# Strassen's scheme in a feed-forward net: seven block products for eight, with the second product run over all rows

## The chip, the cores and the metric

The kernel runs on one core of a Trainium2 chip. The core has five engines that work beside each other, each with its own queue of instructions: TensorE (PE, matrix products into the PSUM memory; PEld is its loading of the stationary operand), VectorE (DVE), ScalarE (ACT), GpSimd (POOL) and SyncE (SP), which here starts all DMA transfers. Data lies in SBUF, 128 partitions, and in PSUM, eight banks of 128 x 512 fp32. The metric is the device time of one execution in microseconds.

## The reference, cut to what matters

One layer on 1024 tokens of width 1024, all in float32: chunked attention and a convolution branch, gated and mixed, a layer norm, then a feed-forward net with a causal depthwise convolution of three taps inside it, and a second layer norm.

```python
def conv_ffn(x, w_up, w_dw, b_dw, w_down):
    u = x @ w_up
    a, b = jnp.split(u, 2, axis=-1)
    a = causal_dwconv(a, w_dw, b_dw)
    return (jax.nn.gelu(a) * b) @ w_down
...
        x = layer_norm(ALPHA * x + mix, ln1_g[l], ln1_b[l])
        ffn = conv_ffn(x, w_up[l], ffn_conv_w[l], ffn_conv_b[l], w_down[l])
        x = layer_norm(ALPHA * x + ffn, ln2_g[l], ln2_b[l])
```

`w_up` is 1024 x 5632 (2 x 2816) and `w_down` 2816 x 1024.

## The kernel before, in words

Float32 products are made of matmuls on a shorter format (fp32r). Each operand is split in two parts: `hi`, a copy on ScalarE into that format, and `lo`, the rest, by a subtraction on VectorE. A product of two blocks is three matmuls, hi x hi, hi x lo and lo x hi (`mm3`, L203 to L206). So all matmuls of the feed-forward net carry the lines L204 to L206, and every block that goes into one costs a copy and a subtraction. Weights come through two rings of raw blocks and of parts (`next_w`, L188 and L189), one block ahead.

`close_tile` makes the layer norm of 128 tokens: `take` adds a bank of the product to the residual `res[t]` (L687), `norm` does the rest (L691 to L710). Tile 7 has a form of its own, with statistics by an instruction of VectorE (L685, L691). `turn(h)` transposes the normed rows of a token half (L743) and splits them (L745, L746).

The feed-forward net follows. Its 22 column tiles f of 128 go in three groups. For each f there are two strips, a and b, each over both token halves with a depth of 8 blocks (`strip`); a gets the three taps (L789 to L791) and gelu (L792), b is multiplied in (L797), and the result is split into the parts `act`. After a group, its part of the down product is added to `res[t]` (L811). The last group closes the tiles: tiles 4 to 7 one after another, with tile 7's second half of columns in two pieces.

The order of the work on each engine isn't that of the lines. The program is given to a planner (`TileContext`), which issues on each engine whatever it expects to be ready, the earlier line first, and puts in the waits; within one engine the order is then fixed. SBUF ranges are handed out in program order by `Arena` (L58): it takes an end of a free range, preferring ranges that were not freed lately. An instruction that writes a range waits for the last reader of what lay there.

## Time and profile before

| | us |
|---|---|
| device time, median of 3 runs | 1447.89 |
| the runs | 1445.92, 1447.89, 1448.00 |
| profiled execution: span from its first to its last instruction | 1445.1 |
| TensorE busy in it | 1433.7 (99%) |
| VectorE, ScalarE, GpSimd busy | 752.9, 480.2, 3.9 |

The page gives the profiled execution no other time than its span; it is 2.8 us below the median of the runs. In rows of instruction groups stand line, engine, operation, output and inputs, count, then busy time, the mean of one in nanoseconds, and the engine's idle time before them with what ended it. In timelines the first number is the start and the second the length.

### The profile page before, as it was taken

To read this page: it belongs to the slowest core of one execution; us is meant where nothing else is said; L and a number is where in the kernel's file an instruction comes from. 1 tells how busy PE (TensorE), PEld (TensorE's weight loads), DVE (VectorE), ACT (ScalarE), POOL (GpSimd) and SP (SyncE) were. 2 spreads that over 40 slices of the span, in tenths; PEclk is the share of its full clock that TensorE was granted. 3 is DMA by queue.
4 is the path that set the end of the run, shared out by engine and by line. 5 is a ranking of instruction groups with operands and counts; after the bars stand their busy time and mean duration, and the time that the engine had idled before them with its cause. 6 is when DMAs were issued, how large, how long until landed. Compare 5 with 4: busy or idle time off the path is not lost.

```text
span 1445.1 us, 15551 instructions
## 1 busy us (share of the span) xinstructions
PE 1433.7 (99%) x6418; PEld 1160.1 (80%) x6418; DVE 752.9 (52%) x1149; ACT 480.2 (33%) x693; POOL 3.9 (0%) x27
## 2 busy tenths in 40 slices
PE   9999999999999999999999999999999999999997
PEld 8877777777778888888888888888888888888886
DVE  5288777786779955756643433213333312333438
ACT  4345455556662137322232222101222200122312
POOL 0000000000000000000000000000000000000000
PEclk9999999999999999999999999999999999999999
DMA  7011111111011111630011111111121111111302
GB/s 255 15 44 39 39 39 39 36 33 39 30 36 38 59 44 34 228 117 1 0 44 44 46 57 44 44 59 45 44 59 44 44 59 44 44 59 44 102 15 117
DMA packets 23285, 80.32 MB, mean 56 GB/s; under 512 B 2592, under 2 KB 2728, under 8 KB 23216
## 3 DMA queue, kind: packets, MB, share of 16 engines
...
q14 instruction: 19, 0.16, 0.0%
...
## 4 chain that ended last, share of the span: by engine, by line
PE 98%; DVE 1%; DMA 0%; ACT 0%; issue 0%; DVEq 0%
PE s L204 18%; PE s L205 18%; PE s L206 18%; PE mm L204 9%; PE mm L205 8%; PE mm L206 8%; PE s L430 2%; PE tp L455 2%; PE s L429 1%; PE tp L204 1%; PE tp L206 1%; PE tp L205 1%; PE pv L204 1%; PE pv L205 1%; PE pv L206 1%; PE pv L477 1%
## 5 line engine op out<-in xcount | busy, mean ns | idle before, releaser
L188 ACT ACTIVATE whi<-wraw 128x1024 fp32r<-128x1024 f32 x100 | 106.1, 1061 | 541.5 <-PE s L205 325.7
L189 DVE TENSOR_TENSOR wlo<-wraw,whi 128x1024 fp32r<-128x1024 f32 x100 | 122.1, 1221 | 310.4 <-ACT whi L188 310.0
L205 PE MATMUL s<-x1l,whi 128*128 128x512 f32 x704 | 274.3, 390 | 0.0
L204 PE MATMUL s<-x1h,whi 128*128 128x512 f32 x704 | 274.1, 390 | 0.0
L206 PE MATMUL s<-x1h,wlo 128*128 128x512 f32 x704 | 274.1, 389 | 0.0
L204 PE MATMUL mm<-xh,whi 128*128 128x512 f32 x384 | 164.3, 428 | 2.0 <-ACT qq L272 2.0
L204 PEld LDWEIGHTS s<-x1h,whi 128*128 128x128 f32 x704 | 132.1, 188 | 27.6 <-ACT x1h L745 0.3
L206 PEld LDWEIGHTS s<-x1h,wlo 128*128 128x128 f32 x704 | 132.2, 188 | 27.3
L205 PEld LDWEIGHTS s<-x1l,whi 128*128 128x128 f32 x704 | 132.1, 188 | 27.2
L412 DVE SCALAR_TENSOR_TENSOR acc<-hpad,par,acc 128x1024 f32<-128x1024 f32 x120 | 152.4, 1278 | 0.7
L206 PE MATMUL mm<-xh,wlo 128*128 128x512 f32 x384 | 151.9, 396 | 0.0
L205 PE MATMUL mm<-xl,whi 128*128 128x512 f32 x384 | 151.5, 394 | 0.0
L797 DVE TENSOR_TENSOR y<-y,s 128x1024 f32<-128x1024 f32 x22 | 26.9, 1221 | 129.1 <-PE s L206 129.1
L204 PEld LDWEIGHTS mm<-xh,whi 128*128 128x128 f32 x384 | 72.2, 188 | 21.7 <-issue 8.2
L206 PEld LDWEIGHTS mm<-xh,wlo 128*128 128x128 f32 x384 | 72.2, 188 | 15.5
L205 PEld LDWEIGHTS mm<-xl,whi 128*128 128x128 f32 x384 | 72.6, 189 | 9.1
L457 ACT ACTIVATE pth<-tp 128x512 fp32r<-128x512 f32 (+3 forms) x96 | 41.7, 434 | 65.2 <-PE tp L455 64.7
L458 DVE TENSOR_TENSOR ptl<-tp,pth 128x512 fp32r<-128x512 f32 (+3 forms) x96 | 46.9, 488 | 30.1 <-ACT pth L457 29.4
L438 ACT ACTIVATE p<-p,st 128x640 f32<-128x640 f32 (+2 forms) x64 | 44.4, 694 | 34.8 <-DVE st L436 34.2
L436 DVE CUSTOM_DVE_ANT_0 p<-s,bias 128x640 f32<-128x640 f32 (+2 forms) x64 | 41.8, 654 | 23.6 <-PE s L430 13.7
L204 PE MATMUL s<-xh,whi 128*128 128x512 f32 x128 | 49.8, 389 | 0.0
L205 PE MATMUL s<-xl,whi 128*128 128x512 f32 x128 | 49.8, 389 | 0.0
...
## 6 DMA issues: line engine op xcount, KB each, us to landing
wraw<-in_w_up SPq DMA_DIRECT2D x44, 512.0 KB, 3.4
wraw<-in_w_in SPq DMA_DIRECT2D x32, 512.0 KB, 3.4
wraw<-in_w_dn SPq DMA_DIRECT2D x22, 512.0 KB, 3.5
res<-in_x SPq DMA_DIRECT2D x8, 512.0 KB, 4.5
wraw<-in_w_o SPq DMA_DIRECT2D x8, 512.0 KB, 3.7
xraw<-in_xT SPq DMA_DIRECT2D x7, 512.0 KB, 7.6
out<-res SPq DMA_DIRECT2D x7, 512.0 KB, 2.6
...
```

What stands on the lines that cost most here:

```text
L188: S.activation(hi, raws[i], AF.Copy)
L189: V.tensor_sub(lo, raws[i], f32(hi))
L204: PE.matmul(o, ah, bh, start=first, stop=False)
L205: PE.matmul(o, ah, bl, start=False, stop=False)
L206: PE.matmul(o, al, bh, start=False, stop=last)
L412: V.scalar_tensor_tensor(a, hp[:, j:j + T], col(C_CW + c * TAPS + j), a, op0=OP.mult, op1=OP.add)
L430: PE.matmul(o[:, b, :w], ql[rs, qs], kk[rs, ks], start=False, stop=True)
L436: V.tensor_tensor_reduce(out=pv, in0=ov, in1=bv, scale=-0.125, scalar=3.0e38, op0=OP.add, op1=OP.min, accum_out=st[:, 0:1])
L438: S.activation(pt, pt, AF.Exp, bias=st[:, 0:1], scale=-1.0, accum_out=st[:, 1:2])
L455: PE.transpose(o[:, (i - i0) * P:(i - i0 + 1) * P], p_t[g][i - 4 * g][:, jj * P:(jj + 1) * P], ident)
L457: S.activation(ph[:, :w], o[:, :w], AF.Copy)
L458: last_lo[0] = V.tensor_sub(pl[:, :w], o[:, :w], f32(ph)[:, :w])
```

## The change

Each matrix of the two products is cut in two by two blocks, and a product of such matrices is made by Strassen's scheme in Winograd's form: seven block products on sums of blocks, and sums of the products. It is done on the blocks before the split into parts.

- The normed rows, transposed, are cut by depth (k blocks 0 to 3 and 4 to 7) and by token half. `turn0` makes the inputs of products 1 and 2 from the first token half, `turn1` those of 4, 5, 7, 6 and 3 from the second and from kept copies of the first. All seven stay in SBUF as parts, 112 KB per partition.
- Up: a `quad` is four weight blocks of 512 rows x 128 columns that belong together. GpSimd makes four sums of the next quad's weights (`prep_sums`), ScalarE and VectorE split weights and sums. Seven products of 12 matmuls follow; some add to the bank of an earlier one, after that one has been read. Results are combined on VectorE and GpSimd. Two quads give two column tiles of a and of b. The taps now read a from SBUF.
- GpSimd makes the four sums of the activations that the down product needs, and all seven inputs go to DRAM (`act_d`); so does the residual (`x1_d`).
- Down: seven products one after another, each over all rows, 11 steps of depth 128 with 12 matmuls each. Each step loads its activations from DRAM through a ring of six, and splits them and its weights (`step_parts`); GpSimd makes sums of weights in place and adds products to the residual. All eight tiles are closed late: tiles 4 to 7 after the sixth product, tiles 0 to 3 within the seventh.
- `close_tile` loses tile 7's own form. `_layout` packs the weights by quads (not shown).

The removed lines that are left out below are the loop over `GROUPS`, L778 to L841; some lines that free ranges are left out too.

```diff
@@ constants and plan @@
-GROUPS = ((0, 8), (8, 16), (16, FT))
+FP = FT // 2
...
-    for f0, f1 in GROUPS:
-        for f in range(f0, f1):
-            plan += [w_up[f], w_up[FT + f]]
-        if f1 < FT:
-            plan += [w_dn[c, f] for c in range(2) for f in range(f0 // 2, f1 // 2)]
-        else:
-            own |= set(range(len(plan), len(plan) + f1 - f0))
-            plan += [w_dn[c, f] for f in range(f0 // 2, f1 // 2) for c in range(2)]
...
@@ close_tile @@
-        r, st, last = res[t], st_r(), t == 7
+        r, st = res[t], st_r()
         m, v, y, z = (st[:, i:i + 1] for i in range(18, 22))
-        at = [0, 0]
-        def take(o):
-            i, a = at
-            n = o.shape[-1]
-            rc = r[:, a:a + n]
-            at[:] = i + 1, a + n
-            if last:
-                V.scalar_tensor_tensor(rc, rc, scale, o, op0=OP.mult, op1=OP.add)
-                V.bn_stats(st[:, 6 * i:6 * i + 6], rc)
+        def take(o, c, sign=None):
+            rc = r[:, cols[c]]
+            if sign is None:
+                V.scalar_tensor_tensor(rc, rc, scale, o, op0=OP.mult, op1=OP.add, accum_out=st[:, c:c + 1])
             else:
-                V.scalar_tensor_tensor(rc, rc, scale, o, op0=OP.mult, op1=OP.add, accum_out=st[:, i:i + 1])
+                V.scalar_tensor_tensor(rc, o, sign, rc, op0=OP.mult, op1=OP.add, accum_out=st[:, c:c + 1])
         def norm():
-            if last:
-                V.bn_aggr(st[:, 18:20], st[:, 0:6 * at[0]])
...
-            for c in cols if last else (slice(0, D),):
...
+            V.scalar_tensor_tensor(r, r, m, g_bc, op0=OP.subtract, op1=OP.mult)
+            V.scalar_tensor_tensor(r, r, y, b_bc, op0=OP.mult, op1=OP.add)
...
@@ build, after close_tiles @@
-    x1t = [[], []]
-    def turn(h):
+    xf = {}
+    xs = {}
+    def part(n):
+        xf[n] = [(sb(f"xfh{n}{i}", [P, HT], F32R), sb(f"xfl{n}{i}", [P, HT], F32R)) for i in range(4)]
+    def turned(o, h, k):
+        for i in range(4):
+            PE.transpose(o[:, toks[i]], res[4 * h + i][:, k * P:(k + 1) * P], ident)
+    def turn0():
+        for n in (1, 2):
+            part(n)
+            xs[n] = [sb(f"xs{n}{i}", [P, HT]) for i in range(4)]
         for k in range(KD):
+            n, i = 1 + k // 4, k % 4
             tp = bank()
-            for i in range(4):
-                PE.transpose(tp[:, toks[i]], res[4 * h + i][:, k * P:(k + 1) * P], ident)
-            hi, lo = sb(f"x1h{h}{k}", [P, HT], F32R), sb(f"x1l{h}{k}", [P, HT], F32R)
+            turned(tp, 0, k)
+            hi, lo = xf[n][i]
             S.activation(hi, tp, AF.Copy)
             V.tensor_sub(lo, tp, f32(hi))
-            x1t[h].append((hi, lo))
+            S.activation(xs[n][i], tp, AF.Copy)
+    def turn1():
+        for n in (4, 5, 7, 6, 3):
+            part(n)
+        for i in range(4):
+            o = bank2()
+            turned(o[:, 0], 1, i + 4)
+            turned(o[:, 1], 1, i)
+            x22, x5, x7, x6, x3 = (sb(f"xs{n}_{i}", [P, HT]) for n in (4, 5, 7, 6, 3))
+            S.activation(x22, o[:, 0], AF.Copy)
+            V.tensor_sub(x5, o[:, 1], x22)
+            V.tensor_sub(x7, xs[1][i], o[:, 1])
+            G.tensor_sub(x6, x5, xs[1][i])
+            G.tensor_add(x3, x6, xs[2][i])
+            for n, a in ((4, x22), (5, x5), (7, x7), (6, x6), (3, x3)):
+                hi, lo = xf[n][i]
+                S.activation(hi, a, AF.Copy)
+                V.tensor_sub(lo, a, f32(hi))
+            sb.free(x22, x5, x7, x6, x3)
+        sb.free(*xs[1], *xs[2])
+    quad_r, quads = [], []
+    wt = []
+    def load_quad():
+        q = len(quads)
+        if q < 2 * FP:
+            quads.append(quad_r[q % len(quad_r)])
+            nc.sync.dma_start(quads[-1], w_up[q])
+    def pair_of_parts(name, n):
+        return sb(name + "h", [P, n, HT], F32R), sb(name + "l", [P, n, HT], F32R)
+    def parts_of(dst, src):
+        hi, lo = dst
+        S.activation(hi, src, AF.Copy)
+        V.tensor_sub(lo, src, f32(hi))
+    def prep_raw(q):
+        if q < 2 * FP:
+            parts_of(wr, quads[q][:, 1:4])
+    def prep_sums(q):
+        if q < 2 * FP:
+            b, t = quads[q], wt[0]
+            G.tensor_add(t[:, 0], b[:, 1], b[:, 0])
+            G.tensor_add(t[:, 1], b[:, 2], b[:, 0])
+            G.tensor_add(t[:, 2], t[:, 0], b[:, 2])
+            G.tensor_add(t[:, 3], t[:, 2], b[:, 3])
+            if q:
+                load_quad()
+    def product(o, w, slot, n, first):
+        for i in range(4):
+            wh, wl = (a[:, slot, i * P:(i + 1) * P] for a in w)
+            xh, xl = xf[n][i]
+            go = first and i == 0
+            PE.matmul(o, wh, xh, start=go, stop=False, skip_group_check=not first)
+            PE.matmul(o, wl, xh, start=False, stop=False, skip_group_check=not first)
+            PE.matmul(o, wh, xl, start=False, stop=i == 3, skip_group_check=not first)
...
+        if t == 4:
+            for r in (raw_r, whi_r, wlo_r):
+                r.close()
+            quad_r.append(sb("quad0", [P, 4, HT]))
+            load_quad()
+            wr = pair_of_parts("wr", 3)
+            prep_raw(0)
         if t == 5:
-            turn(0)
+            turn0()
+    x1_d = [tc.dram_tile([P, D], F32, name=f"x1_d{t}") for t in range(8)]
+    for t in range(4):
+        nc.sync.dma_start(x1_d[t], res[t])
+        sb.free(res[t])
     for a in wo + mix[1]:
         sb.free(*a)
     sb.free(g_bc, b_bc)
-    turn(1)
...
+    wt.append(sb("wt", [P, 4, HT]))
+    w13 = pair_of_parts("w13", 2)
+    w24 = pair_of_parts("w24", 2)
+    prep_sums(0)
+    parts_of(w13, wt[0][:, 0:2])
+    parts_of(w24, wt[0][:, 2:4])
+    turn1()
+    quad_r.append(sb("quad1", [P, 4, HT]))
+    for t in range(4, 8):
+        nc.sync.dma_start(x1_d[t], res[t])
+        sb.free(res[t])
+    a_r = Ring("a", 2, [P, 2 + T])
+    for t in a_r.t:
+        G.memset(t[:, 0:2], 0.0)
+    y_r = Ring("y", 4, [P, T])
+    tmp = {n: sb(f"u{n}", [P, HT]) for n in ("1", "3", "U", "e", "21", "12", "22", "5", "6", "7", "8")}
+    act_d = [{n: tc.dram_tile([P, HT], F32, name=f"act_d{n}_{j}") for n in range(1, 8)} for j in range(FP)]
+    h0, h1 = cols
+    def quad(q, take11, dst21, dst12, dst22):
+        if q % 2 == 0:
+            oa, od = bank(), bank()
+        else:
+            oa, od = (ps_t.tile([P, HT], F32, tag="tp", name="tp"), ps_v.tile([P, HT], F32, tag="pv", name="pv"))
+        cb = bank2()
+        oc, ob = cb[:, 0], cb[:, 1]
+        prep_sums(q + 1)
+        product(oa, wr, 0, 1, True)
+        S.activation(tmp["1"], oa, AF.Copy)
+        product(od, wr, 1, 3, True)
+        S.activation(tmp["3"], od, AF.Copy)
+        product(oa, wr, 2, 2, False)
+        take11(oa)
+        prep_raw(q + 1)
+        product(od, w13, 0, 5, False)
+        product(oc, w13, 1, 7, True)
+        V.tensor_add(tmp["e"], tmp["3"], oc)
+        if q + 1 < 2 * FP:
+            parts_of(w13, wt[0][:, 0:2])
+        product(ob, w24, 0, 6, True)
+        V.tensor_add(tmp["U"], tmp["1"], ob)
+        V.tensor_sub(dst12, od, tmp["U"])
+        G.tensor_sub(dst22, dst12, tmp["e"])
+        product(oc, w24, 1, 4, False)
+        V.tensor_add(dst21, tmp["U"], oc)
+        if q + 1 < 2 * FP:
+            parts_of(w24, wt[0][:, 2:4])
+    load_quad()
+    for j in range(FP):
+        f2 = (j, j + FP)
+        a2 = [a_r(), a_r()]
+        y2 = [y_r(), y_r()]
+        quad(2 * j, lambda o: S.activation(a2[0][:, 2:2 + HT], o, AF.Copy), a2[0][:, 2 + HT:], a2[1][:, 2:2 + HT],
+             a2[1][:, 2 + HT:])
+        for f, a, y in zip(f2, a2, y2):
+            fw = lambda i: col(C_FW + f * FTAPS + i)
+            S.activation(y, a[:, 2:], AF.Identity, bias=col(C_FB + f), scale=fw(2))
+            V.scalar_tensor_tensor(y, a[:, 1:1 + T], fw(1), y, op0=OP.mult, op1=OP.add)
+            V.scalar_tensor_tensor(y, a[:, 0:T], fw(0), y, op0=OP.mult, op1=OP.add)
             S.activation(y, y, AF.Gelu_apprx_tanh)
+        y0, y1 = y2
+        quad(2 * j + 1, lambda o: V.tensor_mul(y0[:, h0], y0[:, h0], o), tmp["21"], tmp["12"], tmp["22"])
+        V.tensor_mul(y1[:, h0], y1[:, h0], tmp["12"])
+        V.tensor_mul(y0[:, h1], y0[:, h1], tmp["21"])
+        V.tensor_mul(y1[:, h1], y1[:, h1], tmp["22"])
+        a11, a21, a12, a22 = y0[:, h0], y0[:, h1], y1[:, h0], y1[:, h1]
+        G.tensor_sub(tmp["5"], a21, a22)
+        G.tensor_sub(tmp["6"], tmp["5"], a11)
+        G.tensor_sub(tmp["7"], a11, a21)
+        G.tensor_add(tmp["8"], tmp["6"], a12)
+        for n, a in ((1, a11), (2, a12), (4, a22), (5, tmp["5"]), (6, tmp["6"]), (7, tmp["7"]), (3, tmp["8"])):
+            nc.sync.dma_start(act_d[j][n], a)
+    for n in xf:
+        for v in xf[n]:
+            sb.free(*v)
+    a_r.close()
+    sb.free(*tmp.values(), *quad_r, *wt, *wr, *w13, *w24)
+    act_r = Ring("actr", 6, [P, HT])
+    dn = [{} for _ in range(FP)]
+    def load_dn(slot):
+        for j in range(FP):
+            dn[j][slot] = sb(f"dn{slot}_{j}", [P, HT])
+            nc.sync.dma_start(dn[j][slot], w_dn[j, slot])
+    hl = [tuple(sb(f"hl{i}{n}", [P, HT], F32R) for n in ("wh", "wl", "ah", "al")) for i in range(6)]
+    hl_i = [0]
+    def step_parts(n, j, slot):
+        a = act_r()
+        nc.sync.dma_start(a, act_d[j][n])
+        v = hl[hl_i[0] % len(hl)]
+        hl_i[0] += 1
+        wh, wl, ah, al = v
+        S.activation(wh, dn[j][slot], AF.Copy)
+        V.tensor_sub(wl, dn[j][slot], f32(wh))
+        S.activation(ah, a, AF.Copy)
+        V.tensor_sub(al, a, f32(ah))
+        return v
+    def step_mm(o, v, t, first, last, more=False):
+        wh, wl, ah, al = v
+        PE.matmul(o, ah[:, toks[t]], wh, start=first and not more, stop=False, skip_group_check=more)
+        PE.matmul(o, ah[:, toks[t]], wl, start=False, stop=False, skip_group_check=more)
+        PE.matmul(o, al[:, toks[t]], wh, start=False, stop=last, skip_group_check=more)
+    def banks_x():
+        return [bank(), bank(), ps_t.tile([P, HT], F32, tag="tp", name="tp"), ps_v.tile([P, HT], F32, tag="pv", name="pv")]
+    def banks_y():
+        a, b = bank2(), bank2()
+        return [a[:, 0], a[:, 1], b[:, 0], b[:, 1]]
+    def down(n, slot, o, more=False, after=None, tail=0, done=None):
+        head = []
+        for j in range(FP):
+            v = step_parts(n, j, slot)
+            if after is not None:
+                after(j)
+            if j >= FP - tail:
+                head.append((j, v))
+                continue
+            for t in range(4):
+                step_mm(o[t], v, t, j == 0, j == FP - 1, more)
+        for t in range(4):
+            for j, v in head:
+                step_mm(o[t], v, t, j == 0, j == FP - 1, more)
+            if done is not None:
+                done(t)
+    load_dn(1)
+    load_dn(0)
+    res = [sb(f"resb{t}", [P, D]) for t in range(8)]
+    p1 = [sb(f"p1_{t}", [P, HT]) for t in range(4)]
+    p5 = [sb(f"p5_{t}", [P, HT]) for t in range(4)]
+    def add_to(slot, by):
+        def f(j):
+            G.tensor_add(dn[j][slot], dn[j][slot], dn[j][by])
+        return f
+    x = banks_x()
+    down(1, 1, x, after=add_to(1, 0))
+    load_dn(2)
+    for t in range(8):
+        nc.sync.dma_start(res[t], x1_d[t])
+    for t in range(4):
+        S.activation(p1[t], x[t], AF.Copy)
+    y = banks_y()
+    down(5, 1, y, after=add_to(1, 2))
+    load_dn(3)
+    for t in range(8):
+        S.activation(res[t], res[t], AF.Copy, scale=ALPHA)
+    for t in range(4):
+        S.activation(p5[t], y[t], AF.Copy)
+        G.tensor_add(res[t][:, h0], res[t][:, h0], p1[t])
+        G.tensor_add(res[t][:, h1], res[t][:, h1], p5[t])
+        G.tensor_add(res[t + 4][:, h1], res[t + 4][:, h1], p5[t])
+    x = banks_x()
+    for j in range(FP):
+        G.tensor_add(dn[j][0], dn[j][0], dn[j][2])
+    down(6, 1, x, after=add_to(1, 3))
+    for t in range(4):
+        V.tensor_add(p1[t], p1[t], x[t])
+        G.tensor_sub(res[t][:, h1], res[t][:, h1], p1[t])
+        G.tensor_add(res[t + 4][:, h0], res[t + 4][:, h0], p1[t])
+    y = banks_y()
+    down(7, 0, y)
...
+    lns = [close_tile(t, 1.0, g_bc, b_bc, out[t]) for t in range(8)]
+    def take(t, c, o, sign=1.0):
+        lns[t][0](o, c, sign)
+    for t in range(4):
+        V.tensor_add(p5[t], p1[t], y[t])
+        take(t + 4, 1, p5[t], -1.0)
+    x = banks_x()
+    down(2, 3, x)
...
+    for t in range(4):
+        take(t, 0, x[t])
+    down(4, 1, y, more=True)
...
+    for t in range(4):
+        take(t + 4, 0, y[t])
+        lns[t + 4][1]()
+    x = banks_x()
+    def done(t):
+        take(t, 1, x[t])
+        lns[t][1]()
+    down(3, 2, x, tail=5, done=done)
```

More of the change, by code (lines that the diff above doesn't have):

```diff
@@ L717, in close_tiles @@
             take, norm = close_tile(t, *a, out=None if outs is None else outs[t])
-            for o in banks(t):
-                take(o)
+            for c, o in enumerate(banks(t)):
+                take(o, c)
             norms.append(norm)
@@ L814, in build @@
-    for a in x1t[0] + x1t[1]:
-        sb.free(*a)
-    y_r.close()
-    g_bc, b_bc = sb("g2", [P, D]), sb("b2", [P, D])
+    wt.append(sb("wt", [P, 4, HT]))
[10 more added lines that the diff above has]
+    a_r = Ring("a", 2, [P, 2 + T])
@@ L818, in build @@
+    for t in range(4):
[3 more added lines that the diff above has]
+    load_dn(3)
     bcast(g_bc, 2)
     bcast(b_bc, 3)
-    f0, f1 = GROUPS[-1]
-    wd = {}
-    o8 = banks8()
-    for f in range(f0, f1):
-        for c in range(2):
-            if f % 2 == 0:
-                wd[c, f // 2] = next_w()
-            wh, wl = (v[:, cols[f % 2]] for v in wd[c, f // 2])
-            for t in range(4):
-                mm3(o8[2 * t + c], act[f][0][:, toks[t]], act[f][1][:, toks[t]], wh, wl, f == f0, f == f1 - 1)
@@ L831, in build @@
-    close_tiles((2, 3, 0, 1), lambda t: o8[2 * t:2 * t + 2], 1.0, g_bc, b_bc, outs=out)
-    for t in range(4, 8):
-        take, norm = close_tile(t, 1.0, g_bc, b_bc, out[t])
-        for i, (a, n) in enumerate(((0, HT), (HT, HT)) if t < 7 else ((0, HT), (HT, HT // 2), (HT + HT // 2, HT // 2))):
-            o = single(t, i)[:, :n]
-            for f in range(f0, f1):
-                wh, wl = wd[a // HT, f // 2]
-                cs = slice(f % 2 * HT + a % HT, f % 2 * HT + a % HT + n)
-                mm3(o, act[f][0][:, toks[t]], act[f][1][:, toks[t]], wh[:, cs], wl[:, cs], f == f0, f == f1 - 1)
-            take(o)
-        norm()
+    for t in range(8):
+        S.activation(res[t], res[t], AF.Copy, scale=ALPHA)
@@ new lines, in build @@
+    y = banks_y()
+    down(7, 0, y)
+    for j in range(FP):
+        sb.free(dn[j][0])
+    lns = [close_tile(t, 1.0, g_bc, b_bc, out[t]) for t in range(8)]
[6 more added lines that the diff above has]
+    down(2, 3, x)
+    for j in range(FP):
+        sb.free(dn[j][3])
+    for t in range(4):
+        take(t, 0, x[t])
+    down(4, 1, y, more=True)
+    for j in range(FP):
+        sb.free(dn[j][1])
```

66 lines of the change are left out of this document (16 added, 50 removed).

## The prediction

> **What bounds the kernel now.** The page comes first: engine busy times, the slices, the chain that ended last.
>
> ```profile
> span 1445.1 us, 15551 instructions
> PE 1433.7 (99%) x6418; PEld 1160.1 (80%) x6418; DVE 752.9 (52%) x1149; ACT 480.2 (33%) x693; POOL 3.9 (0%) x27
> ...
> PE   9999999999999999999999999999999999999997
> ...
> PEclk9999999999999999999999999999999999999999
> ...
> PE 98%; DVE 1%; DMA 0%; ACT 0%; issue 0%; DVEq 0%
> ```
>
> TensorE is never without work, at full clock, and the chain is matmuls for 98% of the span. A busy PE need not be a PE at its peak, so the rate is taken from a period. In the up product one feed-forward tile f takes 2 x 2 x 8 x 3 = 96 matmuls of 512 columns, and ScalarE's first pass over the taps (L789) comes once per tile (timeline of ScalarE, start first):
>
> ```profile
> 1012.89 1.19 ACT L789 ACTIVATE y<-s,par 128x1024 f32<-128x1024 f32 x1
> ...
> 1034.65 1.19 ACT L789 ACTIVATE y<-s,par 128x1024 f32<-128x1024 f32 x1
> ```
>
> 21.76 us for 96 matmuls is **0.2267 us each**. The whole up product is then 22 x 21.76 = 479 us and down 1056 x 0.2267 = 239 us: half of the span is what the change touches. The stretches of the up product show what else is in use (PE, PEld, DVE, ACT, POOL, clock, DMA share, GB/s):
>
> ```profile
> 1000.00:1100.00 100.00, 100.00 (x443) 82.81 (x442) 32.69 (x27) 24.53 (x24) 0.00 (x0) 1.00 0.16 48
> ```
>
> VectorE is free for two thirds, ScalarE for three quarters, GpSimd wholly, DMA mostly. The other thing to know is whether a queue is issued in the order of the lines. TensorE's timeline in the layer norm says no:
>
> ```profile
> 692.89 0.39 PE L204 MATMUL tp<-woh,mxh 128*128 128x512 f32 x1
> 693.12 0.40 PE L205 MATMUL tp<-wol,mxh 128*128 128x512 f32 x1
> 693.35 0.62 PE L743 MATMUL mm<-ident,res 128*128 128x128 f32 x4
> 693.73 0.47 PE L206 MATMUL tp<-woh,mxl 128*128 128x512 f32 x1
> ```
>
> Transposes stand inside another tile's accumulation: the order is a planner's, by when it expects inputs. So a late operand is hidden wherever independent work exists, and a stall is to be looked for only at seams, where none exists.
>
> **The change part by part.** *Removed matmuls.* Up: 22 quads x 7 products x 12 = 1848 against 2112. Down: 7 products x 11 steps x 12 = 924 against 1056 (the last tile's half-width matmuls counted as whole ones). 396 fewer x 0.2267 = **-89.8 us**. Shape and type are the old ones, so is the rate; 64 transposes stay 64.
>
> *Steady state of up.* A pair of quads is 168 matmuls, 38.1 us. The prices of the other engines:
>
> ```profile
> L188 ACT ACTIVATE whi<-wraw 128x1024 fp32r<-128x1024 f32 x100 | 106.1, 1061 | 541.5 <-PE s L205 325.7
> L189 DVE TENSOR_TENSOR wlo<-wraw,whi 128x1024 fp32r<-128x1024 f32 x100 | 122.1, 1221 | 310.4 <-ACT whi L188 310.0
> ...
> L746 DVE TENSOR_TENSOR x1l<-mm,x1h 128x512 fp32r<-128x512 f32 x8 | 5.4, 691 | 2.6 <-ACT x1h L745 2.6
> L745 ACT ACTIVATE x1h<-mm 128x512 fp32r<-128x512 f32 x8 | 4.7, 598 | 5.8 <-PE mm L743 5.6
> L412 DVE SCALAR_TENSOR_TENSOR acc<-hpad,par,acc 128x1024 f32<-128x1024 f32 x120 | 152.4, 1278 | 0.7
> ```
>
> VectorE per pair: weight parts 2 x (1.8 + 1.22 + 1.22) = 8.5 (1.8 for 1536 columns by the 1024 row), four taps 5.1, twelve half-width combinations and products x 0.69 = 8.3; sum 21.9. ScalarE: parts 2 x 3.7, five copies x 0.6, four wide passes x 1.1; sum 14.8. GpSimd: 14 additions of 128x512, which no row shows. The nearest rows:
>
> ```profile
> masks.py:199 POOL TENSOR_SCALAR_AFFINE_SELECT ident<-ident 128x128 f32<-128x128 f32 x1 | 0.4, 357 | 0.0
> ...
> L244 POOL MEMSET eps<- 128x1 f32 x1 | 0.1, 100 | 0.0
> ```
>
> From below 0.69 (VectorE's own). (357 - 100)/127 = 2.0 ns an element gives 0.1 + 1.03 = 1.13 us with one input read; doubled for two inputs, 2.2 us as the upper end. 1.13 is taken, as it comes from that engine: 15.8 us per pair. All three stay under 38.1. The one tight handoff is the sum e = tmp3 + product 7, which must be read from its bank before product 4 adds to it; product 6 covers 12 x 0.2267 = 2.72 us. In the odd quad of a pair the taps (5.1 with ScalarE in turns), the next parts and a product stand before it on VectorE. Bounds 0 and 20 us (1.8 per pair, one wide VectorE instruction late); **+5** is taken, nearer to nothing, since some 13 us of products pass before it is due.
>
> *Seam before up.* The old code enters up on the tokens that are ready; now every product but 1 and 2 needs both halves. After the last matmul of tile 7 comes the norm, now of the longer form; tile 6 shows it (start, length):
>
> ```profile
> 709.62 0.69 DVE L687 SCALAR_TENSOR_TENSOR res<-res,mm 128x512 f32<-128x512 f32 x1 [4.74 <-PE mm L206]
> ...
> 710.54 0.15 DVE L694 TENSOR_SCALAR st<-st 128x1 f32<-128x1 f32 x1
> ...
> 714.15 1.28 DVE L708 SCALAR_TENSOR_TENSOR res<-res,st,b 128x1024 f32<-128x1024 f32 x1
> ```
>
> 5.8 us, plus 0.5 for transposes and 0.6 for the copy x22. Then VectorE does 7 x 0.69 = 4.8 us for each of four k blocks, 19.3 in all, and the sums of quad 0 (2 x 1.22) compete: part 3, last in its list, is whole some 28.7 us after tile 7's last matmul. TensorE can meanwhile do products 1, 2, 6, 7 and three quarters of 3, 57 x 0.2267 = 12.9, and 3.5 us of transposes: 12.3 us are lost. Quad 1's buffer lies, by the allocator's rule, where the kept copies of part 2 were, so its 1 MB load starts only after the last GpSimd addition; about 7 us of load and 3.4 of splitting against 6.1 us of remaining products add 1.7. **+14** (bounds 5, if the planner fills better, and 24, with GpSimd at 2.2).
>
> *Seam from up to down.* Down's first step reads buffers that come free early, but the allocator puts the act buffers of steps 1 and 2 on the last pair's y1. That is read until the last GpSimd addition (tmp8): 0.69 + 0.69 on VectorE and four dependent additions, 4.5 us, after the last product. Then a load and a split. Loads of `before`:
>
> ```profile
> res<-in_x SPq DMA_DIRECT2D x8, 512.0 KB, 4.5
> ...
> xraw<-in_xT SPq DMA_DIRECT2D x7, 512.0 KB, 7.6
> ...
> out<-res SPq DMA_DIRECT2D x7, 512.0 KB, 2.6
> ```
>
> 2.6 us in quiet, 7.6 in a backlog, and there is one: weights, residual and stored activations are all asked for here on the same queue. With 4.5 and 1.3 for the split, step 1 is ready some 12 us after the last product, and step 0 covers 2.7. The clock also falls in such a gap: PE's last matmul of `before` starts at 1436.87, and
>
> ```profile
> 1436.87 0.28 PE L206 MATMUL mm<-woh,act21l 128*128 128x256 f32 x1
> ...
> 1442.00:1445.00 3.00, 0.00 (x0) 0.00 (x0) 0.00 (x0) 0.00 (x0) 0.00 (x0) 0.50 0.45 175
> ```
>
> it is 0.50 five us later. **+11** (bounds 2 and 20).
>
> *Steady state of down.* A step is 12 matmuls, 2.72 us, against two splits on VectorE 1.38, two copies on ScalarE 1.2, one GpSimd addition 1.13 and a load of 256 KB, 96 GB/s (the first microseconds moved 417):
>
> ```profile
> 10.00:12.00 2.00, 2.00 (x10) 1.68 (x9) 1.93 (x3) 1.68 (x3) 0.00 (x0) 1.00 1.04 417
> ```
>
> Six sets of parts give five steps of lead. Hidden, **0**; if that cover goes, up to 20 us.
>
> *Tail.* Before, TensorE ended 8 us before the span, and the last instruction of VectorE 3.2 before it:
>
> ```profile
> 1440.45 1.41 DVE L708 SCALAR_TENSOR_TENSOR res<-res,st,b 128x512 f32<-128x512 f32 x2
> ```
>
> A closing tile costs VectorE 0.69 + 2 x 1.28 and nine column instructions of about 0.15 (L694 in the rows of tile 6 above), 4.6 us. In product 3 all eight tiles close: 36.8 us, and the splits are 11 x 1.38 = 15.2, five steps of them done ahead (6.9). VectorE needs 45 us where TensorE needs 132 x 0.2267 = 29.9. With the 3.2 us for the store, 48.2 against 29.9 + 8: **+10** (bounds 1, the chain of the last tile alone, and 17).
>
> Sum: -89.8 + 5 + 14 + 11 + 0 + 10 = -49.8. On the profiled span 1445.1 gives 1395.3; the runs' median, 1447.89, is 2.8 longer, and that is carried over: **1398 us**.
>
> **The rivals.** *Seams hidden.* The planner finds work for both seams and interleaves the closings: -89.8 + 12 gives about 1370. For it: 99% busy through every seam of `before`. Against it: the sums worked out above leave TensorE no independent products.
>
> *Turn-taking.* VectorE instructions with two SBUF inputs and GpSimd's additions might not run beside each other. Then they add up: per pair 15.7 us (splits 8.5, taps 5.1, three products 2.1) + 14p, p being one addition, against 38.1; in down's products 1, 5, 6 and 7, 44 steps x 1.38 = 60.7 + 64p (11 + 11 + 12 + 11 + 11 + 8 additions) against 4 x 29.9 = 119.7. At p = 1.13 up still fits (31.5) and down is 13 us late, 1411; at 1.5 it is 37 late, 1435. For it: nothing in `before`, where GpSimd adds nothing; against it: nothing either. A page does speak for it, and so against the change: the Trainium skill, SBUF — State Buffer, section "Who interferes with whom", says that a VectorE instruction with two SBUF inputs and a GpSimd instruction that reads SBUF exclude each other for their whole length. By that rule the sum at 1.13 would be the 1411, without it the 1398; no run here shows it yet.
>
> *Slower: GpSimd becomes the bound.* One mechanism, the same sums at a dearer addition. The gain of 49.8 is used up from p = 1.63 us (down 45 late, up at 38.5, 5 late in all); at p = 2.2 it is 11 x 8.4 + 82 = 174, or 1572 us. For it: the upper bound of p. Against it: turn-taking and a slow addition must both hold.
>
> *It doesn't do what it says.* If the new operand order ran at another rate, 2772 matmuls x 0.2267 would change by 6.3 us per 1%. Against it: in `before` the matmul that changes the moving operand (L205) and the one that changes the weights (L206) last as long as the first:
>
> ```profile
> L205 PE MATMUL s<-x1l,whi 128*128 128x512 f32 x704 | 274.3, 390 | 0.0
> L204 PE MATMUL s<-x1h,whi 128*128 128x512 f32 x704 | 274.1, 390 | 0.0
> L206 PE MATMUL s<-x1h,wlo 128*128 128x512 f32 x704 | 274.1, 389 | 0.0
> ```
>
> **How the numbers follow.** The forecast has 0.55 (its own range 1380 to 1410), hidden seams 0.17, turn-taking 0.15, GpSimd as the bound 0.10, another rate or no change 0.03. The range runs from 1366, just below hidden seams, to 1437, the top of turn-taking and of both seams at their bounds (1398 + 10 + 9 + 15 for up = 1432); what is left out is GpSimd as the bound and a few hundredths at each end. 0.2% of the time, 2.9 us, is about what can be told from no change. Faster takes all of the first three: 0.87; slower 0.11; same 0.02.
>
> **What would show it.** The matmul count falls by some 400 and a pair of quads takes 38.1 us; if it takes more, the first release of PE's waits tells whether the addition e or GpSimd is late. TensorE is idle about 12 us before the first quads and about 9 before down's step 1, waiting for parts. In the last 50 us VectorE is full and TensorE waits for splits. A GpSimd addition is near 1.1 us. The prediction is wrong if stalls are spread over the pairs, if down's products take more than 30 us each, or if the seams show no idle PE.

## The result and the profile after

The changed kernel takes **1415.33 us** (median of 4 runs, 1414.33 to 1417.19) where the kernel before, on the same chip, took 1447.75. The ratio is 0.9781, with an interval from 0.9768 to 0.9795: 2.2% faster. The forecast was 1398, so 32.4 us were gained where 49.8 had been expected. The profiled spans differ by the same 32.5 us (1445.1 and 1412.6), and the sums below go by these.

The page of the kernel after, its first two parts and the first line of its chain:

```profile
span 1412.6 us, 16024 instructions
PE 1364.5 (97%) x6004; PEld 1085.9 (77%) x6004; DVE 974.6 (69%) x1387; ACT 614.8 (44%) x924; POOL 362.5 (26%) x255
...
PE   9999999999999999999978999999999995999996
...
PEclk9999999999999999999979999999999997999998
...
PE 90%; DVE 4%; POOL 2%; DMA 1%; issue 1%; ACT 1%; SPq 0%; POOLq 0%; DVEq 0%; ACTq 0%
```

TensorE has two holes now, at the 21st and 22nd slice (the seam before up) and at the 34th (the seam from up to down), and its granted clock dips in both. The chain that was 98% TensorE is 90%. TensorE's waits, longest first, by instruction (total us, times, longest), say who was late:

```profile
PE mm L957 <- ACT hl1ah L951: 15.7, 1, 15.7
PE s L730 <- DVE res L691: 2.9, 1, 2.9
PE s L806 <- ACT xfh L762: 2.2, 1, 2.2
```

and those of its weight loads, which stand in front of a matmul's own wait, show one that comes again in every quad:

```profile
PEld s L806 <- DVE uU L890: 8.0, 22, 1.5
PEld s L806 <- DVE ue L886: 7.0, 20, 1.3
```

**Where the time went.** In TensorE's timeline each matmul of 512 columns should start 0.2267 us after the one before. What the starts lie apart beyond that, added up by stretch, is time that TensorE lost. That gives the account below; the same sum from 713 us to the end of the matmuls is 0.9 us in the kernel before.

| stretch (us of the span after) | us | forecast |
|---|---|---|
| matmuls removed, 396 x 0.2267 | -89.8 | -89.8 |
| seam before up, 713 to 770 | 25.5 | 14 |
| up, 770 to 1145 | 7.0 | 5 |
| seam from up to down, 1145 to 1200 | 21.8 | 11 |
| down, 1200 to TensorE's end | 0.2 | 0 |
| from TensorE's end to the span's end, 12.4 against 8.0 | 4.4 | 10 |
| lost in the same work before | -0.9 | |
| sum | -31.8 | -49.8 |

The measured difference is -32.5; 0.6 of the 0.7 us between lies ahead of the first seam, where tile 7's last matmul starts at 713.15 us in the changed kernel and at 713.72 in the one before. The two seams lost 22.3 us more than forecast and the tail 5.6 less.

**The seam before up.** VectorE's timeline (start, length): the take of the last tile, the end of its norm, and a first block of 128 features from one L756 to the next:

```profile
714.60 0.67 DVE L672 SCALAR_TENSOR_TENSOR res<-res,pv 128x512 f32<-128x512 f32 x1
715.39 1.22 DVE L783 TENSOR_TENSOR w24l<-wt,w24h 128x1024 fp32r<-128x1024 f32 x1
...
720.25 1.28 DVE L691 SCALAR_TENSOR_TENSOR res<-res,st,b 128x1024 f32<-128x1024 f32 x1
723.59 0.69 DVE L756 TENSOR_TENSOR xs<-s,xs 128x512 f32<-128x512 f32 x1 [2.05 <-ACT xs L755]
...
724.79 4.87 DVE L763 TENSOR_TENSOR xfl<-xs,xfh 128x512 fp32r<-128x512 f32 x5
729.58 0.68 DVE L756 TENSOR_TENSOR xs<-s,xs 128x512 f32<-128x512 f32 x1
```

Two of the forecast's lengths are longer here. From the take to the end of the norm it is 6.9 us, not 5.8, as the split w24l and the norm of tile 6 stand between. A block takes 6.0 us (723.59 to 729.58), not 4.8: its five splits, L763, take 4.87 us, though such instructions start only 0.6 us apart where nothing holds them (the two before, 723.59 to 724.79). GpSimd's two additions per block run at that time. The granted clock adds to the loss: it is 0.50 from 725 to 735 us, and matmuls for which the profile shows no wait start up to 0.43 us apart there. Added up over the seam, such distances make some 6 of the 25.5 us (an estimate from the starts).

**The seam from up to down.** TensorE's last matmul before the gap (already one of down's step 0) and the first after it, GpSimd's additions, the loads that SyncE issues, and ScalarE's copy:

```profile
1174.30 0.39 PE L959 MATMUL pv<-hl0wh,hl0al 128*128 128x512 f32 x1
1190.40 0.79 PE L957 MATMUL mm<-hl1wh,hl1ah 128*128 128x512 f32 x1 [15.71 <-ACT hl1ah L951]
```

```profile
1176.40 1.64 POOL L917 TENSOR_TENSOR u<-y,y 128x512 f32<-128x512 f32 x1 [2.73 <-DVE y L914]
...
1180.89 1.25 POOL L995 TENSOR_TENSOR dn<-dn,dn 128x512 f32<-128x512 f32 x1
1182.11 1.25 POOL L920 TENSOR_TENSOR u<-u,y 128x512 f32<-128x512 f32 x1
...
1183.77 1.87 SPq L937 DMA_DIRECT2D dn<-in_w_dn  x4
1185.68 1.38 SPq L945 DMA_DIRECT2D actr<-act_d  x3
...
1189.71 0.63 ACT L951 ACTIVATE hl1ah<-actr 128x512 fp32r<-128x512 f32 x1 [1.82 <-DMA actr<-act_d]
```

The chain is the one that was forecast, link by link: the additions up to L920, which reads y1 last; then SyncE's loads into y1's place; then the copy hl1ah. Each link is longer. An addition of down's weights (L995) stands between two of the last pair's; four weight loads go out ahead of the activations; and down's step 0, which was to cover 2.7 us of the chain, was already done inside the last quad. The granted clock (third figure from the right) falls in the gap:

```profile
1175.00:1190.00 15.00, 0.00 (x0) 0.00 (x0) 6.04 (x7) 2.24 (x5) 10.20 (x8) 0.62 0.72 253
```

**Down.** Its windows (us, PE, PEld, DVE, ACT, POOL, clock, DMA share, GB/s) and two groups of the first:

```profile
1200.00:1290.00 90.00, 90.00 (x399) 74.53 (x398) 89.09 (x68) 47.52 (x80) 76.68 (x47) 1.00 0.50 162
1290.00:1350.00 60.00, 60.00 (x267) 49.67 (x266) 40.43 (x69) 25.43 (x44) 3.58 (x3) 1.00 0.37 106
```

```profile
L995 POOL TENSOR_TENSOR dn<-dn,dn 128x512 f32<-128x512 f32 x25 | 42.0, 1691 | 8.2 <-DVE hl2wl L950 2.5 <-DVE hl1wl L950 1.9 <-DVE hl4wl L950 1.3
L950 DVE TENSOR_TENSOR hl2wl<-dn,hl2wh 128x512 fp32r<-128x512 f32 x6 | 10.5, 1746 | 1.7 <-ACT hl2wh L949 1.7
```

VectorE is full for the 90 us in which GpSimd adds, its splits take 1.45 us on average (the 63 that start in these 90 us; hl2wl's, in the row above, 1.75) where such a split took 0.69 before, and TensorE still never waits. Full VectorE with no price is what the experiments had to explain.

**The tail.** VectorE's takes of the last two tiles, and SyncE's last stores:

```profile
1398.81 0.67 DVE L674 SCALAR_TENSOR_TENSOR resb<-tp,resb 128x512 f32<-128x512 f32 x1
1402.64 0.67 DVE L674 SCALAR_TENSOR_TENSOR resb<-pv,resb 128x512 f32<-128x512 f32 x1
```

```profile
1405.18 3.68 SPq L693 DMA_DIRECT2D out<-resb  x2
```

A closing tile takes 3.83 us (1398.81 to 1402.64), not 4.6, and the list of TensorE's waits has no split from 1365 us on; its weight loads waited 0.5 us in all for two of them.

### The profile page after: what moved, and what is told of

It is laid out like the page before. It is cut to its first block, busy times and chain, and to the rows that moved or that the text cites. A ratio compares the mean times of both kernels' runs of the same rounds, so it can differ in the third digit from the quotient of the medians.

```text
span 1412.6 us, 16024 instructions
## 1 busy us (share of the span) xinstructions
PE 1364.5 (97%) x6004; PEld 1085.9 (77%) x6004; DVE 974.6 (69%) x1387; ACT 614.8 (44%) x924; POOL 362.5 (26%) x255
## 4 chain that ended last, share of the span: by engine, by line
PE 90%; DVE 4%; POOL 2%; DMA 1%; issue 1%; ACT 1%; SPq 0%; POOLq 0%; DVEq 0%; ACTq 0%
PE mm L196 8%; PE mm L197 7%; PE mm L198 7%; PE s L197 5%; PE s L198 5%; PE s L196 5%; PE s L806 4%; PE s L808 4%; PE s L807 4%; PE mm L807 3%; PE mm L808 3%; PE mm L806 3%; PE s L422 2%; PE s L959 2%; PE s L958 2%; PE s L957 2%
## 5 line engine op out<-in xcount | busy, mean ns | idle before, releaser
L794 POOL TENSOR_TENSOR wt<-quad 128x512 f32<-128x512 f32 x22 | 28.4, 1292 | 467.0 <-PE mm L198 373.4
L180 ACT ACTIVATE whi<-wraw 128x1024 fp32r<-128x1024 f32 x40 | 42.4, 1060 | 107.7 <-PE s L197 55.9
L783 DVE TENSOR_TENSOR wrl<-quad,wrh 128x1536 fp32r<-128x1536 f32 x22 | 42.7, 1941 | 59.5 <-ACT wrh L782 59.5
L806 PE MATMUL s<-xfh,w24h 128*128 128x512 f32 x176 | 73.5, 418 | 2.1 <-DVE uU L890 1.1
L808 PE MATMUL s<-xfl,w24h 128*128 128x512 f32 x176 | 69.0, 392 | 0.0
L807 PE MATMUL s<-xfh,w24l 128*128 128x512 f32 x176 | 68.7, 390 | 0.0
L181 DVE TENSOR_TENSOR wlo<-wraw,whi 128x1024 fp32r<-128x1024 f32 x40 | 48.8, 1220 | 21.0 <-ACT whi L180 20.8
L995 POOL TENSOR_TENSOR dn<-dn,dn 128x512 f32<-128x512 f32 x33 | 53.9, 1643 | 24.2 <-DVE hl2wl L950 11.7
L908 DVE SCALAR_TENSOR_TENSOR y<-a,par,y 128x1024 f32<-128x1024 f32 x22 | 38.7, 1758 | 29.5 <-ACT y L907 29.5
L907 ACT ACTIVATE y<-a,par 128x1024 f32<-128x1024 f32 x22 | 27.4, 1245 | 65.8 <-POOL a L892 60.4
```

Source lines behind the costliest of these rows:

```text
L181: V.tensor_sub(lo, raws[i], f32(hi))
L783: V.tensor_sub(lo, src, f32(hi))
L806: PE.matmul(o, wh, xh, start=go, stop=False, skip_group_check=not first)
L807: PE.matmul(o, wl, xh, start=False, stop=False, skip_group_check=not first)
L808: PE.matmul(o, wh, xl, start=False, stop=i == 3, skip_group_check=not first)
L995: G.tensor_add(dn[j][slot], dn[j][slot], dn[j][by])
```

## The experiments

The theory at their start: the loss is at the two seams and in one wait per quad. The seams are chains through VectorE, GpSimd and loads, which are longer than forecast because VectorE and GpSimd hold each other up; elsewhere TensorE's work covers that. The rivals: turn-taking costs the steady state; or the seams are queues and loads and have nothing to do with it. Unless a diff says otherwise, everything else is as in the changed kernel. What TensorE lost in each is in the table, by the rule and the stretches above (us); each ratio is to the kernel before on the same chip. The expectations of the later runs quote the losses with the bounds at 765 and 1150, which left out waits that lie across a bound, 2 to 5 us of them; the table has them.

| kernel | time | ratio to before | seam before up | up | seam to down | down |
|---|---|---|---|---|---|---|
| changed | 1415.33 | 0.9781 (0.9768-0.9795) | 25.5 | 7.0 | 21.8 | 0.2 |
| e_banks | 1405.72 | 0.9717 (0.9702-0.9731) | 25.5 | 0.0 | 19.9 | 0.2 |
| e_narrow | 1398.47 | 0.9662 (0.9648-0.9677) | 16.2 | 6.6 | 15.3 | 0.2 |
| e_dve | 1406.58 | 0.9720 (0.9706-0.9735) | 19.9 | 6.8 | 18.9 | 0.2 |
| e_ring | 1413.43 | 0.9767 (0.9751-0.9783) | 25.6 | 7.2 | 13.7 | 7.3 |
| e_ring_q | 1417.03 | 0.9786 (0.9770-0.9803) | 25.6 | 6.6 | 8.4 | 16.7 |
| e_ring_dve | 1392.08 | 0.9621 (0.9605-0.9637) | 19.9 | 7.2 | 4.2 | 0.2 |
| e_all3 | 1383.26 | 0.9554 (0.9540-0.9568) | 16.7 | -0.1 | 3.8 | 0.2 |

**The two engines by themselves (e_port).** Behind the last line of the changed kernel seven blocks, each started by a sum over what came before:

```diff
+    def gate():
+        V.tensor_add(pa, vo, go)
+        V.tensor_add(pa, pa, ao)
...
+    v2 = lambda: V.tensor_sub(vo, vo, pa)
+    v2p = lambda: V.tensor_sub(vo, vo, pq)
+    v1 = lambda: V.tensor_scalar(vo, vo, 0.5, None, op0=OP.mult)
+    a1 = lambda: S.activation(ao, ao, AF.Copy, scale=0.5)
+    g2 = lambda: G.tensor_sub(go, go, pa)
+    g1 = lambda: G.tensor_scalar(go, go, 0.5, None, op0=OP.mult)
+    both(N, v2, None)
+    both(N, None, g2)
+    both(N, v2, g2)
+    both(N, v2p, g2)
+    both(N, v1, g2)
+    both(N, None, g2, a1)
+    both(N, v2, g1)
```

N is 14, pq lies in PSUM, all else in SBUF.

> Behind the changed kernel's end stand six blocks of work that no result needs, one after another, each of 14 instructions of 128x512 per engine: VectorE subtractions with two inputs in SBUF alone; GpSimd subtractions alone; both; GpSimd with VectorE reading one input from PSUM; GpSimd with VectorE reading one input only; GpSimd with ScalarE copies; last VectorE's two-input subtractions with one-input instructions of GpSimd. Theory (turn-taking): alone 0.69 and 1.27 us each; in the block with both, the two engines' 14 + 14 instructions take about 14 x (0.69 + 1.27) = 27 us; with one input in PSUM, one input only, or ScalarE, the block takes 14 x 1.27 = 18 us. Rival (the long rows in the net were waits for other reasons): the block with both takes 18 us too, and all rows have their length of alone.

The blocks on the two engines' timelines: VectorE alone, GpSimd alone, both, both with an input of VectorE in PSUM, both with one input on VectorE, and, last of each, both with one input on GpSimd:

```profile
1411.27 10.13 DVE L1087 TENSOR_TENSOR vo<-vo,pa 128x512 f32<-128x512 f32 x14
...
1444.49 22.65 DVE L1087 TENSOR_TENSOR vo<-vo,pa 128x512 f32<-128x512 f32 x14
...
1470.20 10.06 DVE L1088 TENSOR_TENSOR vo<-vo,s 128x512 f32<-128x512 f32 x14
...
1491.40 18.91 DVE L1089 TENSOR_SCALAR vo<-vo 128x512 f32<-128x512 f32 x14
...
1534.61 12.43 DVE L1087 TENSOR_TENSOR vo<-vo,pa 128x512 f32<-128x512 f32 x14
```

```profile
1423.86 18.68 POOL L1091 TENSOR_TENSOR go<-go,pa 128x512 f32<-128x512 f32 x14
...
1445.00 23.25 POOL L1091 TENSOR_TENSOR go<-go,pa 128x512 f32<-128x512 f32 x14
...
1470.72 18.73 POOL L1091 TENSOR_TENSOR go<-go,pa 128x512 f32<-128x512 f32 x14
...
1491.91 19.52 POOL L1091 TENSOR_TENSOR go<-go,pa 128x512 f32<-128x512 f32 x14
...
1535.13 23.25 POOL L1092 TENSOR_SCALAR go<-go 128x512 f32<-128x512 f32 x14
```

VectorE alone takes 0.72 us per subtraction, GpSimd 1.33 with its start. Together a pair takes 23.25 / 14 = 1.66 us: more than GpSimd alone, less than the 2.05 of strict turns, so some 0.4 us of the two overlaps. With one input in PSUM neither engine notices the other, nor with ScalarE's copies, where GpSimd again took 18.71 us. The expectation was wrong in one point: an instruction of VectorE with one SBUF input is held too, 1.35 us each where a copy of that size took 0.42 alone (the multiplication itself was not run alone). In the last block the hold is weak: beside GpSimd's one-input multiplication a subtraction of VectorE takes 0.89 us (12.43 / 14) where it took 0.72, though each multiplication takes some 1.5 us. Turn-taking of VectorE's two-input instructions with GpSimd's two-input additions, the pair that the kernel has, is shown, at 1.66 us a pair, where the prediction's rival had 0.69 + 1.13 = 1.82. The rule of the Trainium skill, SBUF — State Buffer, section "Who interferes with whom", which the prediction named, agrees on the subtraction pair, on the input in PSUM, on ScalarE and on VectorE's one-input form (the page's two-port modes). An exclusion "for the whole instruction" is more than was measured: it would make the pair 2.05 us, not 1.66, and the 0.89 us beside GpSimd's one-input multiplication would be at least that instruction's 1.5.

**What turn-taking costs the kernel (e_narrow).** Every GpSimd addition of the feed-forward net works on 8 of its 512 columns, and the other 504 are left out; GpSimd sets the buffers to zero beforehand (not shown):

```diff
+        def tensor_add(self, o, a, b):
+            G.tensor_add(o[:, 0:8], a[:, 0:8], b[:, 0:8])
...
-            G.tensor_sub(x6, x5, xs[1][i])
+            N.tensor_sub(x6, x5, xs[1][i])
```

> The GpSimd additions of the feed-forward net take 8 columns where they took 512, into buffers that were set to zero before; each is still issued, waited for and waiting as before, but it takes some 0.1 us and reads almost nothing, so the sums that come out of them are wrong and the output with them. Theory (what VectorE's longer rows cost is paid at the two seams alone): VectorE's rows go back to 0.69, 1.22 and 1.28 us; a block of 128 features at the first seam takes 4.8 us in place of 6.0 and TensorE loses 5 to 7 us less there; the last additions of the last quad are over 4 to 6 us sooner, so that the second seam loses 4 to 6 us less; up keeps its 38.8 us a pair and down its 0.2 us lost; the time falls by 8 to 13 us. Rival 1 (turn-taking costs the steady state of up): a pair goes to 38.1 us, the time falls by 16 us or more. Rival 2 (the seams are bound by something else, norms, loads and ScalarE): it falls by less than 4 us.

16.9 us faster than the changed kernel: more than the theory's 13, as much as its first rival's 16. But the table says where, and there it is the theory: 9.3 at the first seam, 6.5 at the second, 0.4 in up, nothing in down. The blocks of the first seam (VectorE's timeline):

```profile
728.62 0.68 DVE L766 TENSOR_TENSOR xs<-s,xs 128x512 f32<-128x512 f32 x1
...
732.85 0.68 DVE L766 TENSOR_TENSOR xs<-s,xs 128x512 f32<-128x512 f32 x1
```

4.23 us where it was 6.0. So the two GpSimd additions of a block cost VectorE 0.9 us each, 7 us in four blocks. Up's waits stay, in the list of the weight loads' waits, so these are not turn-taking's:

```profile
PEld s L816 <- DVE ue L902: 7.1, 21, 1.2
PEld s L816 <- DVE uU L906: 6.4, 22, 0.3
```

What is measured here is turn-taking and the additions' own length together; the second seam's chain holds both. The narrow additions were not as short as expected (wt's last two 0.66 us on average), so a little of the effect may still be in this run.

**Up's waits (e_banks).**

```diff
-        cb = bank2()
-        oc, ob = cb[:, 0], cb[:, 1]
+        if q % 2 == 0:
+            cbs[:] = [bank2(), bank2()]
+        oc, ob = (b[:, q % 2] for b in cbs)
```

> Products 4 and 7 of a quad accumulate in one pair of banks and product 6 in another, where all three used two halves of one pair. Theory (up loses 0.35 us per quad because product 6 waits for the addition e, which reads the other half of the same pair, and product 4 for the addition U likewise, with only four matmuls of the next quad as cover): both waits vanish from the list of TensorE's waits, a pair of quads takes 38.1 us where it took 38.8, and the time falls by 6 to 9 us, to about 1408. Rival (the 0.7 us per pair come from additions that VectorE and GpSimd make each other late with): the waits stay or move to other lines, a pair stays at 38.8, and the time is within 2 us.

9.6 us faster. Both waits are gone from the list, and GpSimd's first addition of a pair, which comes once in 168 matmuls, shows the period; the changed kernel first, then e_banks:

```profile
862.32 2.20 POOL L917 TENSOR_TENSOR u<-y,y 128x512 f32<-128x512 f32 x1 [2.13 <-DVE y L914]
901.12 2.20 POOL L917 TENSOR_TENSOR u<-y,y 128x512 f32<-128x512 f32 x1 [2.13 <-DVE y L914]
```

```profile
860.75 2.20 POOL L920 TENSOR_TENSOR u<-y,y 128x512 f32<-128x512 f32 x1 [2.13 <-DVE y L917]
898.84 2.20 POOL L920 TENSOR_TENSOR u<-y,y 128x512 f32<-128x512 f32 x1 [2.13 <-DVE y L917]
```

38.80 us became 38.09, which is 168 x 0.2267. A product that writes one half of a two-bank tile waits for the reader of the other half. All 7.0 us of up's loss are gone by this edit alone, with every GpSimd addition in its place. The first seam kept its 25.5 us, though products 6 and 7 ran sooner: the time came back at the start of the second quad, where a product on tp waits 4.9 us for ScalarE's copy u, which is late through GpSimd's sums.

**No additions on GpSimd (e_dve).** From the token parts on, all 18 lines of this kind:

```diff
-            G.tensor_sub(x6, x5, xs[1][i])
-            G.tensor_add(x3, x6, xs[2][i])
+            V.tensor_sub(x6, x5, xs[1][i])
+            V.tensor_add(x3, x6, xs[2][i])
```

> Every addition that GpSimd does in the feed-forward net goes to VectorE; GpSimd then adds nothing there. Theory (VectorE and GpSimd take turns, but outside the seams this lies under TensorE's work): VectorE's splits in down go back to 0.69 us and the taps to 1.28, up stays at 38.8 us a pair (VectorE gets 14 x 0.69 = 9.7 us more per pair and has the room), the seam before up stays as it is (nine instructions of 0.69 = 6.2 us per block of 128 features against 6.0), the seam from up to down is shorter by 3 us as the last four additions take 0.69 each; the time falls by 2 to 6 us. Rival 1 (turn-taking is what up and the seams lose by): it falls by more than 12 us. Rival 2 (VectorE becomes the bound, with 85% of its time used in up): it rises by 5 us or more.

8.8 us faster, more than the 2 to 6 of the theory, less than its rival's 12. Up loses 6.8 us as before although nothing takes turns there. The first seam gains 5.6, where none was expected: nine instructions 0.6 us apart are 5.4 us, not 6.2, and the second quad's sums are done sooner. The second seam gains 2.9. VectorE is not the bound: it does what GpSimd did, and TensorE loses no more for it.

**The buffers of the second seam (e_ring).**

```diff
+    free_xf(1)
+    act_r = Ring("actr", 6, [P, HT])
+    free_xf(3, 2, 5)
+    hl = [tuple(sb(f"hl{i}{n}", [P, HT], F32R) for n in ("wh", "wl", "ah", "al")) for i in range(6)]
+    free_xf(7, 6, 4)
...
     load_dn(1)
+    a_r.close()
+    y_r.close()
+    sb.free(*tmp.values(), *quad_r, *wt, *wr, *w13, *w24)
     load_dn(0)
```

> Only the buffers at the seam from up to down move: the six activation buffers, the parts of the steps and the first weights of down lie where the token parts of the early products of the last quad were, not where y0 and y1 were. Theory (TensorE's 15.7 us gap is a chain: last addition of the last quad on y1, then loads into y1, then a split): the gap goes, TensorE loses 2 to 5 us at the seam where it lost 21.6, and the time falls by 15 to 19 us, to about 1398. Rival 1 (the gap is a backlog of loads and of one queue, whatever buffers they fill): the wait moves to another load, and the time falls by less than 6 us. Rival 2 (GpSimd and VectorE are simply late there): as rival 1, with TensorE waiting for a split of VectorE and not for a copy.

A miss: 1413.43, not to be told from the changed kernel. The gap of 15.7 us is gone, and the time with it came back in two places: TensorE's waits from 1145 us on.

```profile
PE mm L957 <- ACT hl0ah L951: 6.3, 1, 6.3
...
PE s L958 <- DVE hl4wl L950: 0.8, 2, 0.4
```

Six steps of down ran at once; then the second use of the buffers waited 6.3 us for a load, and down itself, which had lost 0.2 us, lost 7.3, part of it to splits of VectorE. SyncE's queue shows the first of these:

```profile
1183.13 6.68 SPq L922 DMA_DIRECT2D act_d<-u  x4
1189.90 3.74 SPq L938 DMA_DIRECT2D dn<-in_w_dn  x8
1193.69 1.93 SPq L945 DMA_DIRECT2D actr<-act_d  x4
```

The load for step 6 stands behind the last pair's stores and eight loads of weights; the stores wait for GpSimd's additions, and these for VectorE.

**The loads on another queue (e_ring_q).**

```diff
-        nc.sync.dma_start(a, act_d[j][n])
+        nc.scalar.dma_start(a, act_d[j][n])
```

> The buffers as in e_ring, and down's activations are loaded from ScalarE's queue, where e_ring loads them from SyncE's. Theory (in e_ring the loads of the second round of buffers stand behind the last pair's seven stores in SyncE's queue, which wait for GpSimd's last additions, so the gap of the first round came back as one of 6.3 us and many small ones): the 6.3 us wait goes, the seam loses 4 us or less, the time falls to 1398 to 1403. Rival 1 (the DMA engines are full, 0.97 to 1.04 of their time in the stretches of the gap): the waits stay on loads, the time stays within 4 us of e_ring's 1413. Rival 2 (GpSimd and VectorE are late for down's splits, whatever is loaded): TensorE's waits in down name VectorE's splits, the time stays too.

The 6.3 us wait is gone, as the theory had it, and the seam lost 8.4 us, more than the theory's 4; but down lost 16.7 and the time did not fall. Its timelines, TensorE and ScalarE:

```profile
1236.59 0.50 PE L959 MATMUL s<-hl2wh,hl2al 128*128 128x512 f32 x1 [1.17 <-DVE hl2al L952]
...
1241.21 0.50 PE L959 MATMUL s<-hl3wh,hl3al 128*128 128x512 f32 x1 [1.18 <-DVE hl3al L952]
```

```profile
1236.57 0.33 ACTq L945 DMA_DIRECT2D actr<-act_d  x1
1236.99 0.63 ACT L949 ACTIVATE hl3wh<-dn 128x512 fp32r<-128x512 f32 x1 [3.48 <-DVE hl2al L952]
```

A step takes 4.62 us, not 2.72. Two things add up here. VectorE's splits have their 1.8 us of turn-taking; and the edit made a wait of its own, since ScalarE now holds its copies until VectorE's split has freed the buffer that the load goes into. In the step that ends here VectorE stood idle for 1.13 us until ScalarE's copy came (1236.53 to 1237.66), and its two splits then took 3.49 us (to 1241.15), more than TensorE's 2.72 by themselves. How the 16.7 us divide over all steps was not added up.

**The three edits together (e_all3), and without the banks (e_ring_dve).** The diffs are those above.

> The three edits together: the buffers of e_ring, the banks of e_banks, all additions on VectorE as in e_dve. Theory (each takes away a wait of its own, and with the additions on VectorE the last pair's stores leave early enough for e_ring's buffers to help): up loses 2 us, the second seam 2 to 5 us in place of 21.6, the first 15 to 19; the time is 1380 to 1388. Rival 1 (the gains overlap, as e_ring's did with what stood behind it): 1395 to 1405, with a gap of 10 us or more left at the second seam. Rival 2 (VectorE, now 85% busy in up, becomes late without the banks' old slack): above 1405.

> The buffers of e_ring and the additions on VectorE, without the banks of e_banks: which of the two others let e_ring's edit pay in e_all3? Theory (turn-taking did hold it back: with GpSimd adding, the last pair's stores leave late and VectorE is late for down's splits, so that without the gap the same time is lost a little later): the second seam and down lose 4 us together where e_ring lost 18.7, up keeps e_dve's 7.5 lost and the first seam 19; the time is e_all3's 1383 and 10 us for these, 1391 to 1396. Rival (the banks were what mattered, e_ring's buffers are worth 2 us in any company): 1402 to 1406, with 10 us or more lost at the second seam.

1383.26 and 1392.08 us: both theories hold. Alone, e_banks was worth 9.6, e_dve 8.8 and e_ring 1.9, 20.3 in all; together 32.1. The 12 us more are e_ring's, which paid where GpSimd did not add and not beside its additions: on top of e_dve it is worth 14.5 (1406.58 to 1392.08), and the second seam and down lose 4.4 us together where e_ring had lost 21.0. Whether it is the sooner stores or VectorE's free time that makes it pay, e_ring_dve does not separate. e_all3 is 4.5% faster than the kernel before. What it still loses is mostly the first seam, 16.7 us, and the 12.4 us after TensorE's end.

## Why the prediction was right, and where not

**Direction and count: right.** 396 matmuls fell away at 0.2267 us each; e_banks' period of 38.09 us for 168 shows the unchanged rate. The time lies in the stated range, 17 us above the forecast and above the forecast's own 1380 to 1410; 1411, turn-taking's figure at 1.13 us an addition, is nearer, though the loss was not where that rival had it. An addition of GpSimd, 1.13 us in the prediction, took 1.26 alone (the mean of e_port's 14) and 1.59 beside VectorE's subtractions.

**Steady state of up, 5 us forecast, 7.0 measured: the size nearly, the mechanism not.** The step "product 6 covers 12 x 0.2267 = 2.72 us" failed. Product 6 itself waited for e, since its bank is the other half of the tile that e reads, and product 4 for U; only four matmuls of the next quad covered each. e_banks shows it: without the shared tile nothing is lost. By the prediction's own sign (wrong if stalls are spread over the pairs) this part was wrong: the 7.0 us are some 0.64 in each of the 11 pairs.

**Seam before up, 14 forecast, 25.5 measured: mis-sized.** The step "7 x 0.69 = 4.8 us for each of four k blocks" failed: a block is 6.0 us. 1.8 of that is what two GpSimd additions do to VectorE's splits (4.23 us in e_narrow; without them the forecast would have been too long, as instructions in a row start 0.6 us apart). The norm took 6.9, not 5.8. In all, GpSimd's additions cost 9.3 us here by e_narrow, part of it at the second quad's start. The remaining 16.2 are near the forecast's 14, in part by luck: some 6 of them are matmuls at a low clock, for which the sum of this seam had no term. The load of the second quad was not tried by itself; the 1.7 us that the forecast has for it do not follow from the terms beside it (7 + 3.4 - 6.1 is 4.3).

**Seam from up to down, 11 forecast, 21.8 measured: right link by link, too short in each.** From the last product to the end of the additions, 5.9 us in the prediction (0.69 + 0.69 + 4.5): 9.1 us in the trace, from TensorE's last matmul before the gap at 1174.30 to 1183.36. From there to the copy, 4.5 for the load: 6.35 us, 1183.36 to 1189.71. The cover of 2.7 us by step 0 had been spent. With the copy that makes 16.1 us between two starts, 15.9 of them lost. The other 5.9 are 3.1 of waits inside the last quad, which the sum did not have, and 2.7 of matmuls after the gap at a clock of 0.53 (1190 to 1196 us), for which the forecast's 11 had 1.7 above the 9.3 of its chain (12 - 2.7).

**Down, 0 forecast, 0.2 measured: right for a wrong reason.** The cover named was five steps of lead with splits of 0.69 us. They took 1.45, and VectorE was full for 90 us. The gap covered it, since VectorE came out of the seam with its steps ahead. The traces show the lead, from the end of a step's last split to that step's first matmul: in the changed kernel 11.7 us at 1209 us, shrinking to 5.0 at 1299 and never less. e_ring took the gap away: from 1217 us to 1299 its lead is at most 3.4 us and below zero in eight steps, and down lost 7.3 us, part of it on VectorE's splits. e_ring_dve, with the gap and the turns both gone, lost 0.2.

**Turn-taking** had been a rival, worth 13 us and all of it in down. Its mechanism is real (e_port), and with the additions' own length it cost about as much, 15.8 us by e_narrow at the two seams; but its place was wrong. It is paid where VectorE and GpSimd are on TensorE's path, and not where they are merely busy. The forecast had no turn-taking in its sum, and its 1398 is nearly e_narrow's 1398.47; but there too the seams lost 6.5 us more than forecast and up 1.6, most of which the tail gave back.

**Tail, 10 forecast, 4.4: mis-sized.** The closing tile was summed from single lengths; back to back it is 3.83 us, and VectorE had its splits done early enough that TensorE ended without a wait. Those 5.6 us hid a quarter of the misses at the seams.
